# A norm's root made as a row on all partitions in the feed-forward and gate stages of a two-block network

## The chip, the cores and the metric

The kernel runs on one core of a Trainium2 chip. The metric is the device time of one execution in microseconds (us), the median of several runs. The engines are named as the profile names them: PE multiplies matrices, PEld loads its stationary operand, DVE and ACT work on vectors, POOL is GpSimd, SP issues most of the DMAs.

## The reference

A sequence of 256 positions with 1024 features goes through two network blocks. The first has a feed-forward stage, a mixer (neighbourhood attention and pooling), a second feed-forward stage and a gate; the second has a mixer (stick-breaking attention and a convolution), a cross attention to a memory, and a third feed-forward stage. Every stage starts with a norm, and the feed-forward and gate stages look like this:

```python
def rms_norm(x, g):
    xf = x.astype(jnp.float32)
    y = xf * lax.rsqrt(jnp.mean(xf * xf, axis=-1, keepdims=True) + RMS_EPS)
    return (y * g.astype(jnp.float32)).astype(x.dtype)

def swiglu(x, w_gate, w_up, w_down):
    return (jax.nn.silu(x @ w_gate) * (x @ w_up)) @ w_down

f = swiglu(rms_norm(h, ffn1_pre_g[i]), ffn1_w_gate[i], ffn1_w_up[i], ffn1_w_down[i])
h = h + 0.5 * rms_norm(f, ffn1_post_g[i])
...
e = (p[i] @ ple_w_proj[i]) * jax.nn.sigmoid(rms_norm(h, ple_pre_g[i]) @ ple_w_gate[i])
h = h + rms_norm(e, ple_post_g[i])
```

The root is one number for each of the 256 positions. It scales a whole column of a product, so it can be multiplied in after the matmul as well as before it.

## The kernel before

The stream `h` lies transposed in SBUF: features on the 128 partitions in 8 chunks (`DC`), the 256 positions (`T`) along the free axis. Weights come as 345 units of 8 blocks of 128 x 128 floats. `Stream` loads each unit by one DMA into `raw`, ACT rounds it to `wh` (line 90), DVE subtracts to get the remainder `wl` (line 101), and this is issued four units ahead of the unit that PE uses. A product is three matmuls (`mm3`: `wh` by high x, `wl` by high x, `wh` by low x), or two where the moving operand holds both halves of x in 512 columns (`mm2`, `wide`).

Every engine works in the order in which the code issues its instructions; nothing is sorted later. `tick` runs what was put off with `after`. PSUM is five `pm` banks (tile `mm`) and three `pa` banks (tile `at`), taken in turn; a bank is taken again when its last reader is done.

The norm is put off: the matmuls run on `h` times the gain, and the root is multiplied in when a bank is emptied. For it, the squares of the 8 chunks are summed in `acc` (128 x 256). `stat` makes the root as a column: two matmuls of 128 positions each, with one column of ones as the moving operand, put the sums of the positions on partitions; DVE scales 128 x 2 numbers (`v`, line 283), POOL raises them to the power -0.5 (`r`, line 285). `bcast` turns that into a row on all partitions: two matmuls with `r` spread over 128 columns as the stationary operand and the identity as the moving one. `bcast_sb` has ACT copy this row from PSUM to the tile `rs` (line 297).

`ffn` starts with four output pairs at once (`nk` = 4 banks, gate and up half in each) over the 8 chunks. In the last but one chunk (`k == DC - 2`) it calls `stat`; after the last chunk `bcast_sb`, then `evac` four times: DVE multiplies the bank by `rs` (line 445), ACT takes the Silu (line 446), and three later steps make the two halves of `a`. The fifth pair's gate half goes to the fifth bank; its up half needs the first of the four banks again:

```python
            rs = self.bcast_sb(r)
            for m in range(nk):
                evac(m, zt(), bs[m].t)
            for m in range(nk, FC):
                z = zt()
                for sub, (name, off) in enumerate((gate, up)):
                    b = self.bank()
                    self.wide(b, name, off + m, range(DC), x)
```

`ple` (the gate stage) begins likewise with six outputs in three banks, then takes two more in a fourth; `bcast_sb` stands between these two. Its `stages` empty the banks step by step (line 900 multiplies by `rs`) while PE works through `fill`ers, pieces of the memory's key and value products; the last step makes `acc` (line 929) for the `join` behind it, which calls `stat` after four more fillers. `ffn` runs three times, `ple` once. `first_group` in the two mixers, the query stage of the memory, `mem_prep_stat`, `join` and the end of the kernel keep `stat` in both kernels.

The setup allocates a tile `gap` of 128 x 128 floats that nothing uses.

Of the kernel before, what the change touches and what calls it, by code (L numbers as in the profile page):

```python
# [10 lines left out]
F32 = mybir.dt.float32  # L11
F32R = mybir.dt.float32r
AF = mybir.ActivationFunctionType
ALU = mybir.AluOpType

P = 128
T = 256
D = 1024
# [3 lines left out]
EPS = 1e-6  # L22
# [117 lines left out]
class Net:  # L140
# [89 lines left out]
    def setup(self):  # L230
        nc, b, d = self.nc, self.base, self.d
        hg = b.tile([P, G_ALL + DC * T], F32, name="hg")
        self.gv, self.h = hg[:, 0:G_ALL], hg[:, G_ALL:].rearrange("p (c t) -> p c t", c=DC)
        self.x = Split(b.tile([P, DC, 2, T], F32R, name="x"))
        self.fg = b.tile([P, DC, T], F32, name="fg")
        self.ident = b.tile([P, P], F32, name="ident")
        self.ones = b.tile([P, 1], F32, name="ones")
        self.mhalf = b.tile([P, 2], F32, name="mhalf")
        self.half = b.tile([P, 4 * DC], F32, name="half")
        nc.scalar.preload_act_table_set("silu_and_others")  # L240
        at = [(0, 1), (1, 1), (2, 2), (4, 2), (6, 2)]
        for u, (lo, n) in enumerate(at):
            s = slice(G_ALL + lo * T if lo else 0, G_ALL + (lo + n) * T)
            nc.sync.dma_start(out=hg[:, s], in_=d["gx"][:, s])  # L244
            self.ws.load(u, START.get(u, (UB,)))
        nc.gpsimd.memset(self.ones, 1.0)
        nc.gpsimd.memset(self.mhalf, -0.5)
        idle = self.fg[:, 0]
        nc.vector.memset(idle, 0.0)
        w = self.abank()  # L250
        for _ in range(WARM):
            nc.tensor.matmul(w.t[:, 0:T], idle[:, 0:P], idle, start=True, stop=True)
        nc.gpsimd.dma_start(out=self.ident, in_=d["cst"][:, C_ID:C_ID + P])
        b.tile([P, P], F32, name="gap")

    def g(self, name, c):
        i = GAINS.index(name) * DC + c
# [22 lines left out]
    def stat_end(self, b):  # L280
        nc = self.nc
        v = self.tmp.tile([P, 2], F32, tag="v", name="v")
        nc.vector.tensor_scalar(out=v, in0=b.t[:, 0:2], scalar1=1.0 / D, scalar2=EPS, op0=ALU.mult, op1=ALU.add)  # L283
        r = self.tmp.tile([P, 2], F32, tag="r", name="r", bufs=3)
        nc.gpsimd.tensor_tensor(out=r, in0=v, in1=self.mhalf, op=ALU.pow)  # L285
        return r

    def bcast(self, r):

        b = self.abank()  # L290
        for t in range(2):
            self.mm(b, b.t[:, t * P:(t + 1) * P], r[:, t:t + 1].to_broadcast([P, P]), self.ident, stop=True)
        return b.t
# [135 lines left out]
    def ffn(self, gate, up, down, on_chunk, nk=4):  # L429
        nc = self.nc  # L430
        x = self.x
        with self.tc.tile_pool(name="ffn", bufs=1, reuse_waits="tile") as fp:
            self.fp = fp
            a = Split(fp.tile([P, FC, 2, T], F32R, name="a"))
            aH, aL = a[0], a[1]

            def zt():
                return fp.tile([P, 2, T], F32, tag="z", name="z", bufs=6)

            def join2(z, b):  # L440
                nc.scalar.copy(out=z, in_=b.t[:, 1])  # L441
                nc.vector.tensor_tensor(out=z, in0=b.t[:, 0], in1=z, op=ALU.add)  # L442

            def evac(m, z, src):
                nc.vector.tensor_tensor(out=z, in0=src, in1=self.row(rs), op=ALU.mult)  # L445
                nc.scalar.activation(out=z[:, 0], in_=z[:, 0], func=AF.Silu)  # L446

                def s1():
                    nc.vector.tensor_tensor(out=z[:, 0], in0=z[:, 0], in1=z[:, 1], op=ALU.mult)  # L449

                def s2():
                    nc.scalar.copy(out=aH[:, m], in_=z[:, 0])

                def s3():
                    nc.vector.tensor_tensor(out=aL[:, m], in0=z[:, 0], in1=aH[:, m].bitcast(F32), op=ALU.subtract)

                self.after(1, s1)
                self.after(2, s2)
                self.after(3, s3)

            bs = [self.bank() for _ in range(nk)]
            for k in range(DC):
                for m in range(nk):
                    for sub, (name, off) in enumerate((gate, up)):
                        w = self.ws.take(name, k, off + m)
                        self.mm3(bs[m], bs[m].t[:, sub], w, x.at(k), stop=k == DC - 1)
                if k == DC - 2:
                    r = self.stat([self.acc])
                self.tick()
            rs = self.bcast_sb(r)  # L470
            for m in range(nk):
                evac(m, zt(), bs[m].t)
            for m in range(nk, FC):
# [4 lines that stand above are left out]
                    join2(z[:, sub], b)  # L478
                    if sub == 1:
                        evac(m, z, z)  # L480
                    self.tick()
            for c in range(DC):
                b = self.bank()
                two = c < DC - 1
                for k in range(FC):
                    w = self.ws.take(down, k, c)
                    if two:
                        self.mm2(b, w, a.at(k), stop=k == FC - 1)
                    else:
                        self.mm3(b, b.t[:, 0], w, a.at(k), stop=k == FC - 1)  # L490
                    if k % 8 == 4:
                        self.tick()
                on_chunk(c, b.t[:, 0], b.t[:, 1] if two else None)
# [386 lines left out]
    def ple(self, fill):  # L880
        nc = self.nc
        x = self.x
        gp = self.halved(2, "ple_post_g", 0.5)
        bs = [self.bank() for _ in range(3)]
        for k in range(DC):
            for j in range(6):
                w = self.ws.take("ple_w_gate", k, j)
                self.mm3(bs[j // 2], bs[j // 2].t[:, j % 2], w, x.at(k), stop=k == DC - 1)
            if k == DC - 2:
                r = self.stat([self.acc])  # L890
            self.tick()
        fg = self.fg
        qs = []
        off = (0, 0, 0, 1)

        def stage(i, j):
            s = slice(2 * j, 2 * j + 2)
            f = fg[:, s]
            if i == 0:
                nc.vector.tensor_tensor(out=f, in0=bs[j].t, in1=self.row(rs), op=ALU.mult)  # L900
            elif i == 1:
                nc.scalar.activation(out=f, in_=f, func=AF.Tanh, scale=0.5)
            elif i == 2:
                nc.vector.scalar_tensor_tensor(out=f, in0=f, scalar=1.0, in1=self.pp[:, s], op0=ALU.add, op1=ALU.mult)
            elif i == 3:
                q = self.plez.tile([P, 2, T], F32, tag="pq", name="pq", bufs=4)
                nc.scalar.activation(out=q, in_=f, func=AF.Square, scale=0.5)
                qs.append(q)
            elif i == 4:
                if j:  # L910
                    nc.vector.tensor_tensor(out=qs[0], in0=qs[0], in1=qs[j], op=ALU.add)

        def stages(n):
            for j in range(4):
                if 0 <= n - off[j] < 5:
                    stage(n - off[j], j)

        bs.append(self.bank())
        for i in range(2):
            self.proj(bs[3], i, "ple_w_gate", 6 + i, range(DC), x)  # L920
            if i == 0:
                rs = self.bcast_sb(r)
            stages(i)
            self.tick()
        for n in range(2, 6):
            self.fill(fill)
            stages(n)
        self.acc = self.new_acc()
        nc.vector.tensor_tensor(out=self.acc, in0=qs[0][:, 0], in1=qs[0][:, 1], op=ALU.add)
        return gp  # L930
# [532 lines left out]
```

## Time and profile before

| | |
|---|---|
| median of 3 runs | 1034.66 us (1033.92 to 1034.78) |
| the profiled execution's own time | 1036.4 us |
| its span, first to last instruction | 1034.6 us |
| PE busy | 1024.7 us (99%) |
| DVE busy | 760.9 us (74%) |
| ACT busy | 585.1 us (57%) |
| POOL busy | 44.9 us (4%) |
| mean granted TensorE clock | 0.998 |

The span is shorter than the execution's time by 1.8 us. Times in the rows below count from the start of the span. A matmul's record is longer than the matmul's share of PE, since matmuls overlap: what one costs is read from the distance between two starts. An fp32 matmul of the program stands as two records in the trace, one of the rounded kind as one.

### The profile page before, as it was taken

The numbers are of one execution on the slowest core, as the hardware profiler recorded it, in microseconds if no ns is written. First come the engines' busy times: TensorE is split into PE (matmuls) and PEld (weight loads), VectorE is DVE, ScalarE is ACT, GpSimd is POOL, SyncE is SP. The second block draws the span as 40 slices with busy tenths as digits, with TensorE's granted clock in tenths as the row PEclk, the third lists the DMA queues.
The fourth block names the chain that finished last, engine by engine and source line by source line (L and its number), as shares of the span: only waits on it lengthen the run. The fifth ranks groups of instructions, "written<-read, shape, count | busy, mean of one in ns | idle before, by whom it ended". The sixth has DMA issues, their size and how long they took to land.

```text
span 1034.6 us, 18209 instructions
## 1 busy us (share of the span) xinstructions
PE 1024.7 (99%) x7272; PEld 963.9 (93%) x7272; DVE 760.9 (74%) x1200; ACT 585.1 (57%) x981; POOL 44.9 (4%) x73
## 2 busy tenths in 40 slices
PE   9999999999999999999999999999999999999996
PEld 8988888999999998888889999999999999888886
DVE  7798864687858679888457776886678677878652
ACT  7566654464654556556456565465556555656531
POOL 0100000120000110000000111000001000000000
PEclk9999999999999999999999999999999999999999
DMA  8566665455555655666655665555566346666541
GB/s 299 191 218 213 186 206 197 175 191 180 197 162 163 208 203 164 204 187 183 203 183 183 194 201 195 163 163 163 159 222 231 105 140 198 211 187 187 183 156 42
DMA packets 55014, 191.35 MB, mean 185 GB/s; under 512 B 6400, under 2 KB 7936, under 8 KB 54928
## 3 DMA queue, kind: packets, MB, share of 16 engines
q1 hardware_dynamic: 52848, 184.11, 54.7%
q0 software_dynamic: 1936, 5.80, 1.9%
q8 instruction: 57, 0.93, 0.4%
q14 instruction: 29, 0.24, 0.1%
q10 hardware_dynamic: 144, 0.26, 0.1%
HBM read 187.00 MB, written 3.15 MB: 184 GB/s over the span
## 4 chain that ended last, share of the span: by engine, by line
PE 82%; issue 16%; DMA 0%; POOL 0%; DVE 0%; SPq 0%; POOLq 0%; DVEq 0%; ACT 0%
PE mm L197 79%; PE at L197 3%; PE at L875 1%; DMA raw<-ws 0%; POOL r L285 0%; DVE fg L1373 0%; POOLq L1456 0%; DVEq L1456 0%; SPq L63 0%; ACT wh L78 0%; SPq L244 0%; DVE v L283 0%
## 5 line engine op out<-in xcount | busy, mean ns | idle before, releaser
L197 PE MATMUL mm<-x,wh 128*128 128x256 f32 (+1 forms) x2784 | 654.1, 316 | 0.7 <-ACT wh L78 0.7
L197 PE MATMUL mm<-x,wl 128*128 128x256 f32 x1824 | 513.6, 282 | 0.0
L197 PEld LDWEIGHTS mm<-x,wh 128*128 128x128 f32 x2784 | 462.2, 189 | 36.1 <-ACT wh L78 1.6
L101 DVE TENSOR_TENSOR wl<-raw,wh 128x1024 fp32r<-128x1024 f32 x340 | 409.7, 1219 | 11.6 <-ACT wh L90 5.9
L90 ACT CAST wh<-raw 128x1024 fp32r<-128x1024 f32 x340 | 349.0, 1046 | 37.7 <-PE mm L197 22.6
L197 PEld LDWEIGHTS mm<-x,wl 128*128 128x128 f32 x1824 | 345.5, 189 | 1.2 <-DVE wl L79 0.4
L197 PE MATMUL mm<-a,wh 128*128 128x512 f32 (+1 forms) x594 | 185.2, 368 | 0.0
L197 PE MATMUL mm<-a,wl 128*128 128x256 f32 x528 | 147.5, 280 | 0.0
L197 PEld LDWEIGHTS mm<-a,wh 128*128 128x128 f32 x594 | 107.2, 188 | 19.1
L197 PEld LDWEIGHTS mm<-a,wl 128*128 128x128 f32 x528 | 99.2, 188 | 0.0
L446 ACT ACTIVATE z<-z 128x256 f32<-128x256 f32 x66 | 27.2, 418 | 80.6 <-DVE z L445 80.6
L442 DVE TENSOR_TENSOR z<-mm,z 128x256 f32<-128x256 f32 x108 | 45.5, 421 | 29.9 <-ACT z L441 29.8
L441 ACT COPY z<-mm 128x256 f32<-128x256 f32 x108 | 39.6, 367 | 32.9 <-PE mm L197 32.7
L307 ACT ACTIVATE x<-hg 128x256 fp32r<-128x256 f32 x56 | 27.5, 537 | 41.6 <-DVE hg L380 22.1
L285 POOL TENSOR_TENSOR r<-v,mhalf 128x2 f32<-128x2 f32 x13 | 18.5, 1422 | 679.8 <-DVE v L283 679.8
L445 DVE TENSOR_TENSOR z<-z,rs 128x512 f32<-128x512 f32 x54 | 37.4, 692 | 1.8
L352 DVE TENSOR_TENSOR fg<-mm,fg 128x256 f32<-128x256 f32 x14 | 5.9, 425 | 40.7 <-ACT fg L351 40.7
L449 DVE TENSOR_TENSOR z<-z 128x256 f32<-128x256 f32 x66 | 27.2, 424 | 8.1 <-ACT z L446 1.9
L311 DVE SCALAR_TENSOR_TENSOR x<-hg,x 128x256 fp32r<-128x256 f32 x56 | 26.8, 515 | 6.6 <-ACT x L307 6.6
L351 ACT COPY fg<-mm 128x256 f32<-128x256 f32 x14 | 5.2, 373 | 42.0 <-PE mm L197 42.0
L326 DVE TENSOR_TENSOR acc<-acc,sq 128x256 f32<-128x256 f32 x27 | 11.5, 426 | 23.6 <-ACT sq L325 23.5
L197 PE MATMUL mm<-y,wh 128*128 128x256 f32 x136 | 27.7, 283 | 0.0
(218 smaller groups left out, 1033.0 us busy)
## 6 DMA issues: line engine op xcount, KB each, us to landing
raw<-ws SPq DMA_DIRECT2D x340, 512.0 KB, 4.1
raw<-ws SPq DMA_DIRECT2D x9, 256.0 KB, 5.3
ub<-ub SPq DMA_DIRECT2D x8, 160.0 KB, 2.8
mraw<-memT POOLq DMA_DIRECT2D x8, 128.0 KB, 4.3
kd<-kv POOLq DMA_DIRECT2D x8, 128.0 KB, 3.6
vd<-kv POOLq DMA_DIRECT2D x4, 256.0 KB, 4.5
kv<-kd POOLq DMA_DIRECT2D x4, 256.0 KB, 5.9
kv<-vd POOLq DMA_DIRECT2D x4, 256.0 KB, 6.7
```

Of the source, the lines that this page charges most:

```text
L90: self.nc.scalar.copy(out=h, in_=self.R[self.nhigh])
L101: self.nc.vector.tensor_tensor(out=l, in0=self.R.pop(u), in1=self.H[u].bitcast(F32), op=ALU.subtract)
L197: self.nc.tensor.matmul(out, lhsT, rhs, start=not b.started, stop=stop, skip_group_check=True)
L285: nc.gpsimd.tensor_tensor(out=r, in0=v, in1=self.mhalf, op=ALU.pow)
L307: self.nc.scalar.activation(out=self.ordered(x[0][:, c]), in_=self.rows(self.h[:, c]), func=AF.Copy, scale=gain(c))
L311: self.nc.vector.scalar_tensor_tensor(out=l, in0=self.rows(self.h[:, c]), scalar=gain(c), in1=h, op0=ALU.mult, op1=ALU.subtract)
L326: nc.vector.tensor_tensor(out=acc, in0=acc, in1=s, op=ALU.add)
L441: nc.scalar.copy(out=z, in_=b.t[:, 1])
L442: nc.vector.tensor_tensor(out=z, in0=b.t[:, 0], in1=z, op=ALU.add)
L445: nc.vector.tensor_tensor(out=z, in0=src, in1=self.row(rs), op=ALU.mult)
L446: nc.scalar.activation(out=z[:, 0], in_=z[:, 0], func=AF.Silu)
L449: nc.vector.tensor_tensor(out=z[:, 0], in0=z[:, 0], in1=z[:, 1], op=ALU.mult)
```

## The change

`stat_all` is a new function: one matmul has a 128 x 128 square of ones as its stationary operand and `acc` (256 columns) as the moving one, so that the sums of all positions stand as a row on every partition. DVE scales 128 x 256 numbers from PSUM into the tile `rs`, and POOL raises this tile to the power -0.5 in place. `ffn` and `ple` call it in the last but one chunk where they called `stat`, and no longer call `bcast_sb`. The tile of ones takes the place of `gap`, and POOL fills it once in the setup.

```diff
-        b.tile([P, P], F32, name="gap")
+        self.square1 = b.tile([P, P], F32, name="square1")
+        nc.gpsimd.memset(self.square1, 1.0)
...
+    def stat_all(self, a):
+
+        nc = self.nc
+        b = self.abank()
+        self.mm(b, b.t[:, 0:T], self.square1, a, stop=True)
+        t = self.tmp.tile([P, T], F32, tag="rs", name="rs", bufs=1)
+        nc.vector.tensor_scalar(out=t, in0=b.t[:, 0:T], scalar1=1.0 / D, scalar2=EPS, op0=ALU.mult, op1=ALU.add)
+        nc.gpsimd.tensor_tensor(out=t, in0=t, in1=self.mhalf[:, 0:1].to_broadcast([P, T]), op=ALU.pow)
+        return t
...
                 if k == DC - 2:
-                    r = self.stat([self.acc])
+                    rs = self.stat_all(self.acc)
                 self.tick()
-            rs = self.bcast_sb(r)
             for m in range(nk):
...
             if k == DC - 2:
-                r = self.stat([self.acc])
+                rs = self.stat_all(self.acc)
             self.tick()
...
             self.proj(bs[3], i, "ple_w_gate", 6 + i, range(DC), x)
-            if i == 0:
-                rs = self.bcast_sb(r)
             stages(i)
```

What stands on DVE around the norm of the first feed-forward stage, before (`z<-mm,rs` is `evac`'s product with the root, `z<-mm,z` and `z<-z` its later steps):

```order
L101 TENSOR_TENSOR wl<-raw,wh 128x1024 x6
L283 TENSOR_SCALAR v<-at 128x2
L101 TENSOR_TENSOR wl<-raw,wh 128x1024
L445 TENSOR_TENSOR z<-mm,rs 128x512 x4
L101 TENSOR_TENSOR wl<-raw,wh 128x1024
L442 TENSOR_TENSOR z<-mm,z 128x256
```

The same place in the changed kernel:

```order
L101 TENSOR_TENSOR wl<-raw,wh 128x1024 x6
L295 TENSOR_SCALAR rs<-at 128x256
L101 TENSOR_TENSOR wl<-raw,wh 128x1024
L456 TENSOR_TENSOR z<-mm,rs 128x512 x4
L101 TENSOR_TENSOR wl<-raw,wh 128x1024
L453 TENSOR_TENSOR z<-mm,z 128x256
```

The order is the same; the scaling step has 256 columns where it had 2, and one `wl` still stands between it and the four products.

On POOL, from the first DMA of the setup to the second root (`ISA` is the loading of the power's code, `mraw` a chunk of the memory's input), before:

```order
L253 DMA ident<-cst 128x128
L285 ISA
L285 TENSOR_TENSOR r<-v,mhalf 128x2
L501 DMA mraw<-memT 128x256 x8
L285 TENSOR_TENSOR r<-v,mhalf 128x2 x2
```

The same place in the changed kernel:

```order
L253 DMA ident<-cst 128x128
L255 MEMSET square_114 128x128
L296 ISA
L296 TENSOR_TENSOR rs<-rs,mhalf 128x256
L511 DMA mraw<-memT 128x256 x8
L286 TENSOR_TENSOR r<-v,mhalf 128x2 x2
```

The first power now has 256 columns, and the DMAs of `mraw` stand behind it as they stood behind the small one; the other feed-forward stages and the gate read alike.

## Rows read from the trace of the kernel before

**Rows 1.** First section of the page: busy time, share of the span, instructions.

```profile
PE 1024.7 (99%) x7272; PEld 963.9 (93%) x7272; DVE 760.9 (74%) x1200; ACT 585.1 (57%) x981; POOL 44.9 (4%) x73
```

**Rows 2.** Waits of PE, all of them: total us, times, longest.

```profile
PE at L252 <- DVE fg L249: 1.2, 1, 1.2
PE at L197 <- ACT sq L1284: 0.8, 1, 0.8
PE mm L197 <- ACT wh L78: 0.7, 1, 0.7
```

**Rows 3.** Timeline of PE at the first norm: start, length, instruction, records.

```profile
28.86 0.50 PE L197 MATMUL at<-ones,acc 128*128 128x1 f32 x4
29.22 0.36 PE L197 MATMUL mm<-x,wh 128*128 128x256 f32 x1
29.42 0.28 PE L197 MATMUL mm<-x,wl 128*128 128x256 f32 x1
...
32.11 0.61 PE L197 MATMUL at<-ident,r 128*128 128x128 f32 x4
32.47 0.48 PE L197 MATMUL mm<-x,wh 128*128 128x512 f32 x1
32.79 0.28 PE L197 MATMUL mm<-x,wl 128*128 128x256 f32 x1
32.91 0.39 PE L197 MATMUL mm<-x,wh 128*128 128x512 f32 x1
...
34.99 0.39 PE L197 MATMUL mm<-x,wh 128*128 128x512 f32 x1
...
35.33 0.39 PE L197 MATMUL mm<-x,wh 128*128 128x512 f32 x1
```

**Rows 4.** Timeline of PE in the second mixer, an fp32 256-column and 128-column matmul.

```profile
654.47 0.87 PE L197 MATMUL mm<-qz,kT 128*128 128x256 f32 x4
655.09 0.36 PE L197 MATMUL mm<-x,wh 128*128 128x256 f32 x1
```

**Rows 5.** DVE: timeline at the first norm, then one group of lines by form.

```profile
29.39 0.16 DVE L283 TENSOR_SCALAR v<-at 128x2 f32<-128x2 f32 x1 [3.13 <-PE at L197]
29.50 1.23 DVE L101 TENSOR_TENSOR wl<-raw,wh 128x1024 fp32r<-128x1024 f32 x1
33.16 2.49 DVE L445 TENSOR_TENSOR z<-mm,rs 128x512 f32<-128x512 f32 x4 [2.43 <-ACT rs L297]
...
L442 DVE TENSOR_TENSOR z<-mm,z 128x256 f32<-128x256 f32 x108 | 45.5, 421 | 29.9 <-ACT z L441 29.8
```

**Rows 6.** POOL: line 285 (ns min/median/max), its first instruction, two memsets by form.

```profile
L285 POOL TENSOR_TENSOR r<-v,mhalf x13: 692/1600/1661, 29.7 to 1027.2; 128x2 f32<-128x2 f32 x13
...
29.71 1.60 POOL L285 TENSOR_TENSOR r<-v,mhalf 128x2 f32<-128x2 f32 x1 [27.69 <-DVE v L283]
...
L609 POOL MEMSET vz<- 128x512 f32 x4 | 2.2, 608 | 0.0
...
L246 POOL MEMSET ones<- 128x1 f32 x1 | 0.1, 98 | 0.3 <-POOLq L1453 0.3
```

**Rows 7.** The gate stage: timeline of DVE, and PE at the next norm.

```profile
572.02 0.16 DVE L283 TENSOR_SCALAR v<-at 128x2 f32<-128x2 f32 x1 [0.81 <-PE at L197]
572.12 2.36 DVE L101 TENSOR_TENSOR wl<-raw,wh 128x1024 fp32r<-128x1024 f32 x2
577.80 1.89 DVE L900 TENSOR_TENSOR fg<-mm,rs 128x512 f32<-128x512 f32 x3 [3.32 <-ACT rs L297]
...
589.60 0.43 DVE L929 TENSOR_TENSOR acc<-pq 128x256 f32<-128x256 f32 x1
...
592.21 0.50 PE L197 MATMUL at<-ones,acc 128*128 128x1 f32 x4
```

**Rows 8.** DVE, line 101: ns min/median/max of all its instructions.

```profile
L101 DVE TENSOR_TENSOR wl<-raw,wh x340: 1208/1219/1237, 19.1 to 1012.2; 128x1024 fp32r<-128x1024 f32 x170
```

**Rows 9.** Stretches: length, busy us of each engine (records), granted clock, DMA.

```profile
10.00:12.00 2.00, 2.00 (x11) 2.00 (x11) 1.77 (x3) 1.72 (x4) 0.00 (x0) 1.00 1.05 377
26.00:32.00 6.00, 6.00 (x54) 6.00 (x53) 1.60 (x3) 2.10 (x2) 2.29 (x3) 1.00 0.87 310
```

## The prediction

> **What bounds the kernel now.** I read the busy times first: PE is busy 99% of the span, POOL 4% [rows 1]. Then the waits: PE waited three times, 2.7 us in all, never at one of the norms that change [rows 2]. So PE's own work sets the end. A matmul taken off PE is worth its share in full; whatever makes PE wait costs in full; faster work on the other engines is worth nothing. The waits of DVE at these norms [rows 5, 7] cost nothing today, because PE has work meanwhile. What matters is how long the root may take before PE has none.
>
> **PE's work.** There are four places: three feed-forward stages and the gate. I read prices as distances between starts, and count the late start of the matmul behind, since two neighbours are normally 0.12 us apart (32.79 to 32.91) [rows 3]. The two narrow matmuls of the old sum take 29.22 - 28.86 = 0.36 us, and the step behind them is 0.20 in place of 0.12: 0.44. The two broadcast matmuls take 32.47 - 32.11 = 0.36, and the 512-column matmul behind them keeps PE 0.32 where another keeps it 0.23 (34.99 to 35.33 holds a pair, 0.34, less 0.12): 0.45 with rounding. Together 0.89. The new matmul is fp32, 256 columns, with a 128-column stationary operand. Its nearest row is the pair in the mixer: one of 256 and one of 128 columns take 655.09 - 654.47 = 0.62 [rows 4]; half of the broadcast's 0.36 is the share of the 128-column one, so 0.44 is left, and 0.08 for the step behind: 0.52. The saving is 0.37 a place, four times: **1.5 us**. ACT's copy of the row goes too; PE did not wait for it, so it counts as nothing by itself. The 128 x 128 memset in the setup costs POOL, by the memsets [rows 6], under 0.25 us near the start, where POOL then idles 27.69 us until 29.71: nothing. The changed positions of SP's DMAs: none.
>
> **DVE's step.** Scaling 256 columns from PSUM in place of 2: the nearest row is a 256-column step that reads PSUM, 0.42 us [rows 5], against 0.16. That is 0.26 later for the `wl` behind it, which is made four units ahead and hides it.
>
> **The power's price.** With 2 columns it takes 0.69 us where DVE lets it; the median of 1.60 is longer only because of a wait: the first one starts at 29.71, beside a `wl` from 29.50 to 30.73, and ends at 31.31, that is 0.58 after the `wl` [rows 5, 6]. Nothing in the trace has more than 2 columns of it, so the price of one more column, call it c, is bounded from both sides. Lower end: a memset's column, (608 - 98)/511 = 1.0 ns [rows 6]; the power would then take 0.69 + 254 x 0.001 = 0.95 us. Upper end: all of 0.69 beyond the memset's 0.10 of handling belongs to the two columns, 0.295 us each, and 256 of them take 75.6 us. It cannot be a gain. The ends are a factor of 80 apart. The row nearest in kind is the power itself, and it says that 0.59 us lies beyond what handling costs a memset, so the function is not cheap; but two columns also pay once for whatever filling of a pipe there is, so the full upper end is not likely either. I take the geometric middle, sqrt(0.95 x 75.6) = 8.5 us, that is **c = 31 ns** and 254 c = 7.8 us beyond the small power. This is the one number of the forecast that I choose rather than read.
>
> **How much of it is hidden in a feed-forward stage.** Replayed with the rows of the first norm [rows 3, 5, 6]. The new matmul ends 0.08 later than the old pair, so DVE's scaling starts at 29.39 + 0.08 = 29.47 and ends at 29.89. The `wl` behind it starts 0.05 earlier than that (29.50 against 29.55 today), 29.84, and ends at 31.07. The power ends 0.58 after it plus 254 c: 31.65 + 254 c. `evac`'s first product waits for that, takes a fourth of 2.49 with its overlaps, 0.69 us for one (2.49 less three starts 0.60 apart), and frees the first bank at about 32.4 + 254 c. PE, without the broadcast, starts the fifth pair at 32.11 + 0.08 = 32.19; its gate half is 8 pairs of 0.345, (35.33 - 32.47 - 0.10)/8, so PE wants the first bank at 34.95. The wait is 254 c - 2.5 us. The other two feed-forward stages have the same order and the same distances within 0.1 us. With 254 c = 7.8 each waits 5.3, **15.9 us** for three. Queued behind the waiting product: on DVE the other three products and the next `wl`, on ACT the four Silus and the next rounding, on POOL the DMAs of `mraw` and `kv`, wanted much later. The weights are four units ahead, 32 blocks of 0.35 us or 11 us, so this lateness does not add to the wait for the bank; the later banks come free every 0.6 us while PE needs 2.8 for each.
>
> **The gate.** Here the scaling would run from 572.10 to 572.52, the first `wl` to 573.70 and the power to 574.28 + 254 c. DVE's first product stands at 577.80 today, since it waited for the broadcast. From there DVE works nearly without a gap until `acc` at 590.03, and PE asks for it at 592.21 [rows 7], which is 2.2 to spare. So 577.80 + 2.18 - 574.31 = 5.7 us of 254 c are hidden. With 7.8, PE waits **2.1 us**. PE's bank for its second filler comes free earlier than that and is no limit.
>
> One more way to lose time: POOL and DVE can stand in each other's way. The rows show one direction, the power waited for `wl`'s end [rows 5, 6]. The other does not show: all 340 `wl` took 1.208 to 1.237 us, also those that ran beside a power [rows 8]. The Trainium skill, "SBUF — State Buffer", section "SBUF: two separate sides", says that whoever starts first holds the pair for the whole instruction and the other is blocked. By it the gate's second `wl` would stand behind the power and add 1.2 us there; the row speaks against it, and the sum has nothing for it.
>
> **PE's pace after a wait.** At the start of the program PE ran 11 records in 2 us, 5.5 a us, where later it runs 54 in 6, 9.0 a us [rows 9]; the column of the granted clock reads 1.00, the level of 2.4 GHz, in both. If a wait of 5 us brought that slow pace back for as long as the wait was, each would cost 5.3 x 3.5/9.0 = 2.1 us more. No row has a wait inside the work, so the bounds are 0 and 2.1; I take 0, because the clock's column shows no fall, and keep the other end for the range (up to 8 us for four).
>
> **The sum.** 15.9 + 2.1 - 1.5 = +16.5 us. Against the profiled execution's own 1036.4 us (span 1034.6) that is 1052.9; that execution was 1.7 us above the median of the runs, so for a median I add to 1034.66: **1051.1 us**, slower by 1.6%.
>
> **The rivals.** *The power is hidden.* If c is below 2.5/254 = 10 ns, PE never waits and only the 1.5 us remain: 1033.2, not slower. The mechanism is a pipelined power that pays most of its 0.69 us once. For it: DVE's scaling step has the same shape of price, 0.16 us for 2 columns though 256 take only 0.42. Against it: a memset has only 0.10 to pay once. It decides at c = 10 ns; the balance of gain and loss is at 3 (254 c - 2.5) = 1.5, c = 12 ns. The Trainium skill, "GPSIMD Engine Reference", section "Elementwise — side-by-side cycle accounting", gives about 2.6 cycles at 1.2 GHz for an element of a two-input operation, measured for an addition; an estimate by it is 0.55 us for 256 columns, which would be this rival and 1033.2. No run here shows it for a power. *No overlap between columns.* If half of the 0.59 us is paid per column, c = 148 ns, 254 c = 37.5, three waits of 35.0 and one of 31.8: 1034.66 + 136.8 - 1.5 = 1170; at the full upper end, 254 c = 75, it is 1320. For it: a root by logarithm and exponential is long, and two columns took 0.69. *Partly hidden.* c between 10 and 14 ns leaves the time within 0.2%: three waits of 1.2 against 1.5.
>
> **How the numbers follow.** About 0.2%, 2.07 us, is what a measurement of this kernel can tell from no change. Power hidden or nearly so (c up to 14 ns): 0.38, nearly all of it within 0.2%; faster by more than that needs a saving above 2.07 where the rows give 1.5, so 0.04 of it. The forecast's case, c from 14 to 90 ns: 0.46. Beyond: 0.16. That gives faster 0.04, same 0.34, slower 0.62. At c = 90 ns, 254 c = 22.9, the sum is 61.2 + 17.2 - 1.5 = 76.9, and with a slow pace after some of the waits about 81: the range ends at 1115. It starts at 1032.8, the hidden case with 0.4 for reading errors. What is left out is the last case and the fast tail, 2 in 10.
>
> **What would show it.** In the changed profile, the power's row gives c at once. Right: PE waits at three places for DVE's product with `rs`, each 254 c - 2.5, and less at the gate's next norm; DVE's idle time at that line goes to POOL. The saving would show as four pairs of broadcast matmuls gone, and starts of the new matmul 0.44 before the next one. Wrong: a power under 3.2 us and no wait of PE; or waits of PE for `wl`, a slower pace behind a wait, or longer `wl` beside the power.

## The result and the profile after

The changed kernel takes 1187.46 us (median of 5 runs, 1186.59 to 1188.93) against 1034.39 of the kernel before: a ratio of 1.1486, 95% interval 1.1474 to 1.1498. That is 153.1 us more, outside the range that was given. The direction was right, the size was not.

The page of the changed kernel, first section (busy time, share, instructions) and the chain that ended last, to be read beside [rows 1]:

```profile
PE 1030.6 (87%) x7248; PEld 967.1 (81%) x7248; DVE 762.3 (64%) x1200; ACT 584.6 (49%) x977; POOL 206.6 (17%) x74
...
PE 69%; POOL 14%; issue 14%; DVE 1%; DMA 0%; SPq 0%; POOLq 0%; DVEq 0%; ACT 0%
```

PE's busy time hardly moved; it stood still for 13% of the span. POOL works 162 us more, and one line of it is 14% of the chain. The waits of PE in the changed kernel (total us, times, longest), beside [rows 2]:

```profile
PE mm L197 <- DVE z L456: 113.5, 3, 37.9
PE mm L197 <- DVE fg L910: 32.9, 1, 32.9
```

These are the three feed-forward stages and the gate: 146.4 us of waiting that was not there. The power itself (ns min/median/max) and the first of the four places on POOL, DVE and PE, each from its timeline:

```profile
L296 POOL TENSOR_TENSOR rs<-rs,mhalf x4: 41992/41998/42055, 28.5 to 971.5; 128x256 f32<-128x256 f32 x4
...
28.46 42.00 POOL L296 TENSOR_TENSOR rs<-rs,mhalf 128x256 f32<-128x256 f32 x1 [26.20 <-DVE rs L295]
...
70.50 2.49 DVE L456 TENSOR_TENSOR z<-mm,rs 128x512 f32<-128x512 f32 x4 [41.06 <-POOL rs L296]
...
71.33 0.76 PE L197 MATMUL mm<-x,wh 128*128 128x512 f32 x1 [37.91 <-DVE z L456]
72.11 0.63 PE L197 MATMUL mm<-x,wh 128*128 128x512 f32 x1
72.75 0.63 PE L197 MATMUL mm<-x,wh 128*128 128x512 f32 x1
...
75.11 0.39 PE L197 MATMUL mm<-x,wh 128*128 128x512 f32 x1
75.45 0.39 PE L197 MATMUL mm<-x,wh 128*128 128x512 f32 x1
```

256 columns of power take 42.0 us. DVE's product, PE's bank and PE's next matmul follow one behind the other, as the prediction had put it. Behind the wait the pairs of matmuls stand 0.64 us apart, not 0.345, until about 75. The stretches there (length, busy us of PE, PEld, DVE, ACT, POOL with records, then the granted clock, the DMA's share and its GB/s) say why:

```profile
36.00:70.00 34.00, 0.00 (x0) 0.00 (x0) 0.00 (x0) 0.00 (x0) 34.00 (x1) 0.52 0.00 0
...
72.00:74.00 2.00, 2.00 (x8) 1.71 (x7) 2.00 (x3) 1.64 (x4) 0.11 (x1) 0.50 0.63 178
74.00:76.00 2.00, 2.00 (x11) 1.77 (x10) 1.44 (x5) 1.59 (x3) 0.00 (x0) 0.79 0.39 72
76.00:80.00 4.00, 4.00 (x25) 3.54 (x24) 3.48 (x7) 1.71 (x6) 0.00 (x0) 1.00 0.55 177
```

The granted clock fell to 0.50, the level of 1.2 GHz, while PE stood still, and it was still there for the first matmuls.

### The profile page after: what moved, and what is told of

It reads as the page before. It is cut to its first block, busy times and chain, and to the rows that moved or that the text cites. A ratio compares the mean times of both kernels' runs of the same rounds, so it can differ in the third digit from the quotient of the medians.

```text
span 1186.7 us, 18164 instructions
## 1 busy us (share of the span) xinstructions
PE 1030.6 (87%) x7248; PEld 967.1 (81%) x7248; DVE 762.3 (64%) x1200; ACT 584.6 (49%) x977; POOL 206.6 (17%) x74
## 4 chain that ended last, share of the span: by engine, by line
PE 69%; POOL 14%; issue 14%; DVE 1%; DMA 0%; SPq 0%; POOLq 0%; DVEq 0%; ACT 0%
PE mm L197 66%; POOL rs L296 14%; PE at L197 3%; PE at L885 0%; DMA raw<-ws 0%; DVE wl L101 0%; DVE fg L914 0%; DVE fg L910 0%; DVE pq L921 0%; DVE rs L295 0%; POOL r L286 0%; DVE z L456 0%; SPq L63 0%; DVE fg L1381 0%; POOLq L1464 0%
## 5 line engine op out<-in xcount | busy, mean ns | idle before, releaser
L296 POOL TENSOR_TENSOR rs<-rs,mhalf 128x256 f32<-128x256 f32 x4 | 168.0, 42010 | 101.5 <-DVE rs L295 101.5
L286 POOL TENSOR_TENSOR r<-v,mhalf 128x2 f32<-128x2 f32 x9 | 11.9, 1320 | 573.6 <-DVE v L284 573.6
L456 DVE TENSOR_TENSOR z<-mm,rs 128x512 f32<-128x512 f32 x12 | 7.5, 684 | 123.2 <-POOL rs L296 123.2
L197 PE MATMUL mm<-wh,m 128*128 128x256 f32 x128 | 25.5, 297 | 32.9 <-DVE fg L910 32.9
L197 PEld LDWEIGHTS mm<-wh,m 128*128 128x128 f32 x128 | 21.4, 202 | 33.1 <-DVE fg L910 33.1
```

Source lines behind the costliest of these rows:

```text
L197: self.nc.tensor.matmul(out, lhsT, rhs, start=not b.started, stop=stop, skip_group_check=True)
L296: nc.gpsimd.tensor_tensor(out=t, in0=t, in1=self.mhalf[:, 0:1].to_broadcast([P, T]), op=ALU.pow)
```

## The experiments

The theory: all of the loss is the power's price per column, through the waits for the bank and the low clock behind them; the rest of the change is a small gain. The rivals: making the row on POOL costs by itself; the replay of what is hidden was wrong too; the slow pace behind the waits is weights that come late.

**Multiply instead of power.**

```diff
-        nc.gpsimd.tensor_tensor(..., op=ALU.pow)
+        nc.gpsimd.tensor_tensor(..., op=ALU.mult)
```

> The changed kernel with GpSimd's power replaced by a multiplication of the same 256 columns (so the root is left out and the output differs). Theory, the power's price per column is the whole loss and the rest of the change saves 1.5 us on PE: 1032.9 us, no wait of PE at the four places, GpSimd's instruction under 2 us. Rival, the loss lies in making the row on GpSimd at all (its reads beside VectorE, or the wait on one more engine in the chain): still above 1036, with a wait of PE for the product with rs.

Measured: 1032.42 us against 1034.46, a ratio of 0.998 (0.9971 to 0.9988). PE does not wait at any of the four places. Line 296 of this kernel:

```profile
L296 POOL TENSOR_TENSOR rs<-rs,mhalf x4: 609/1450/1512, 28.2 to 856.4; 128x256 f32<-128x256 f32 x4
```

The same columns in the same place on the same engine take 0.61 us when the function is a product: that is the first of the four, which starts before the `wl`; the other three start beside a running `wl` and take 1.45 to 1.51, as the small power did. So POOL, its reads and the further wait in the chain are not the loss; the function is. The first rival falls.

**Powers of four sizes, off the path.**

```diff
-        b.tile([P, P], F32, name="gap")
+        gap = b.tile([P, P], F32, name="gap")
+        nc.gpsimd.memset(gap, 0.7)
+        for n in (2, 2, 16, 64):
+            nc.gpsimd.tensor_tensor(out=gap[:, 0:n], in0=gap[:, 0:n], in1=self.mhalf[:, 0:1].to_broadcast([P, n]), op=ALU.pow)
```

> The kernel before, with four powers that nobody reads in GpSimd's idle time at the start, of 2, 2, 16 and 64 columns in this order. Theory, a fixed part and a constant price per column: 42.0 us for 256 and 0.69 for 2 give 0.163 us a column, so 0.69, 0.69, 3.0 and 10.8 us; the time stays at 1034.4 within 1 us, since nobody waits. Rival, a price that grows in steps or a cost of the first call: 16 columns below 1.5 us, or the first power longer than the second by 1 us or more. Second rival, a power holds back VectorE's two-input instructions for its whole length: wl instructions beside it of 3 to 10 us, and a time above 1036.

Measured: 1034.22 us, ratio 0.9999 (0.999 to 1.0009). POOL's groups by form (busy us, mean ns):

```profile
L257 POOL TENSOR_TENSOR gap<-gap,mhalf 128x64 f32<-128x64 f32 x1 | 10.8, 10797 | 0.1
L257 POOL TENSOR_TENSOR gap<-gap,mhalf 128x16 f32<-128x16 f32 x1 | 2.9, 2948 | 0.1
L257 POOL TENSOR_TENSOR gap<-gap,mhalf 128x2 f32<-128x2 f32 x2 | 1.4, 710 | 0.2
```

From 2 to 16 columns it is (2.948 - 0.710)/14 = 0.160 us a column, from 16 to 64 (10.797 - 2.948)/48 = 0.164: a straight line with some 0.38 us paid once. No cost of the first call shows. The same line gives 42.2 us at 256 columns. Nobody waits for these powers and they cost nothing. The second rival falls too: the eleven `wl` of line 79 ran beside these powers and took 0.43 to 0.69 us, in the kernel before 0.42 to 0.69.

**A power of 48 columns.** It takes nearly the time that the prediction assumed, so it tests everything but the price.

```diff
-        nc.gpsimd.tensor_tensor(out=t, in0=t, in1=self.mhalf[:, 0:1].to_broadcast([P, T]), op=ALU.pow)
+        nc.gpsimd.tensor_tensor(out=t[:, 0:48], in0=t[:, 0:48], in1=self.mhalf[:, 0:1].to_broadcast([P, 48]), op=ALU.pow)
```

> The changed kernel with the power on the first 48 of the 256 columns only (the other columns keep the mean square, so the output differs). At 0.163 us a column this power takes 8.2 us, 7.5 beyond the small one, nearly what the prediction chose. Theory, the prediction's replay of the stages was right and its price was wrong: waits of PE of 5.0 us at three places and about 1.8 at the gate, less 1.5 of saving: 1050, up to 1057 if PE runs slowly behind each wait. Rival, the replay hides less or more than it said (a wait comes 2 us earlier, or the later banks and weights add to it): below 1045 or above 1060.

Measured: 1055.2 us, ratio 1.0201 (1.0187 to 1.0215). The waits of PE in this kernel, and two stretches around the first of them:

```profile
PE mm L197 <- DVE z L456: 14.4, 3, 5.0
PE at L197 <- DVE acc L937: 1.9, 1, 1.9
...
34.00:36.00 2.00, 0.00 (x0) 0.00 (x0) 0.00 (x0) 0.00 (x0) 2.00 (x1) 0.82 0.00 0
...
38.00:40.00 2.00, 2.00 (x8) 1.71 (x8) 1.92 (x3) 1.64 (x4) 0.00 (x0) 0.50 0.50 156
```

Three waits of 4.8 on average where 5.0 were expected, and 1.9 at the gate, for `acc`, where 1.8 were. The waits are 16.3 us; less about 2 of gain that leaves some 14, and 1055.2 - 1034.5 = 20.7 were measured. The rest, some 6.4 us, goes to the clock: it falls within a wait of 5 us too, and from the first matmul behind the first wait the next eight pairs took 5.2 us where they take 2.8, which is 2.4 for a wait and 7.2 for three. The replay of the waits holds.

**PE kept busy during the waits**, first with 155 idle matmuls in each of the three feed-forward waits, then with 166.

```diff
                     self.wide(b, name, off + m, range(DC), x)
+                    if m == nk and sub == 0:
+                        w = self.abank()
+                        for _ in range(155):
+                            nc.tensor.matmul(w.t, x.at(0)[0][:, 0:P], x.at(0)[2].rearrange("p a t -> p (a t)"), start=True, stop=True)
```

> The changed kernel with 155 matmuls of 512 columns, read by nobody, in each of the three feed-forward waits, about 35 us each, so that PE is busy nearly until the power ends. Theory, a wait of 38 us costs a further 1.7 us at each place because TensorE's clock has fallen to 1.2 GHz and comes back only later: 1182.3, the granted clock at 1.00 in the first us behind these three waits, and 0.5 behind the gate's wait, which is left as it is. Rival, PE is slow there for another reason (weights or banks that come late): 1187.5 within 1.5 us, and the same distances between matmuls behind the wait.

> As the run with 155 idle matmuls, with 166 of them. There 2.8 us were left idle behind them, and the granted clock fell all the same, so that run could not tell. Now some 0.4 us stay idle. Theory, the slow pace behind the three feed-forward waits is the granted clock's: 1182.3 us (1187.4 less three times 1.7), pairs 0.345 us apart at once behind the wait, the clock at 1.00 there. Rival, late weights or banks: 1187.4 within 1.5 us and pairs 0.64 us apart behind the wait.

Measured: 1187.4 us with 155, no different from the changed kernel; 1181.54 with 166. The first left 2.8 us idle (three waits, 8.1 us in all), and the clock went down all the same; the second left two waits of 0.2. The stretch of 72 to 74 us, first with 155, then with 166, and behind the second the power at this place and the first two pairs:

```profile
72.00:74.00 2.00, 2.00 (x9) 1.71 (x8) 1.96 (x3) 1.64 (x4) 0.00 (x0) 0.50 0.51 154
```

```profile
72.00:74.00 2.00, 2.00 (x13) 1.76 (x13) 1.44 (x3) 2.00 (x4) 0.00 (x0) 1.00 0.36 55
...
28.00 41.16 POOL L296 TENSOR_TENSOR rs<-rs,mhalf 128x256 f32<-128x256 f32 x1 [25.73 <-DVE rs L295]
...
70.44 0.39 PE L197 MATMUL mm<-x,wh 128*128 128x512 f32 x1
...
70.79 0.39 PE L197 MATMUL mm<-x,wh 128*128 128x512 f32 x1
```

With the clock at 1.00 the pairs stand 0.345 us apart at once, with the same weights and banks, and 5.9 us are gone. In the profiled executions 0.8 of them are the first power's, 41.16 us where it takes 42.00 in the changed kernel: here it starts at 28.00, before the `wl` beside it, there at 28.46, behind the start of the `wl` at 28.22. That leaves 1.7 for each wait, and the starts in the changed kernel say the same: the six pairs from 71.33 to 75.11 take 3.78 us in place of 2.07. So the slow pace is the clock's, and the third rival falls. The first of the two runs could not tell: its expectation was wrong in assuming that so short an idle time would not matter.

**A power of 16 columns.**

```diff
-        nc.gpsimd.tensor_tensor(out=t, in0=t, in1=self.mhalf[:, 0:1].to_broadcast([P, T]), op=ALU.pow)
+        nc.gpsimd.tensor_tensor(out=t[:, 0:16], in0=t[:, 0:16], in1=self.mhalf[:, 0:1].to_broadcast([P, 16]), op=ALU.pow)
```

> The changed kernel with the power on the first 16 columns only (the others keep the mean square, so the output differs). This power took 2.95 us by itself, 2.26 beyond the small one, just below the 2.5 us that the prediction found hidden. Theory: PE never waits at the four places, 1032.4 us, as with the multiplication. Rival, less is hidden than the prediction said: a wait of 0.5 us or more at each place and 1034 or more.

Measured: 1031.69 us, ratio 0.9971 (0.996 to 0.9982), no wait of PE at the four places, though each power, with the `wl` that it waits for, lasts 3.8 us. DVE still waited for them, 10.2 us in all; that cost nothing. Together with 48 columns this brackets the point at which a longer power starts to cost: between 16 and 48 columns, where the prediction's 2.5 us put it at about 17.

**The gate alone.** The feed-forward stages go back to `stat` and `bcast_sb`.

```diff
                 if k == DC - 2:
-                    rs = self.stat_all(self.acc)
+                    r = self.stat([self.acc])
                 self.tick()
+            rs = self.bcast_sb(r)
```

> The change in the gate stage alone; the feed-forward stages are those of before. Theory, the four places add up, and the gate's share is its wait of 32.9 us in the changed kernel's trace, 1.7 us of low clock behind it, less 0.5 of saving: 1068.6 us. By the prediction's own replay, with 5.7 us hidden, 254 columns at 0.163 give 35.7 and 1071.4. Rival, the places are not independent: off by more than 3 us from both.

Measured: 1068.12 us, ratio 1.0325 (1.0311 to 1.0339), with the one wait of 32.9 us. That is what was expected if the places add up. The 1071.4 by the prediction's formula is 3.3 too long; the part on the prediction says why.

**The root by ScalarE from the same row.** Does the row form gain where the root is quick?

```diff
-        nc.vector.tensor_scalar(out=t, in0=b.t[:, 0:T], scalar1=1.0 / D, scalar2=EPS, op0=ALU.mult, op1=ALU.add)
-        nc.gpsimd.tensor_tensor(out=t, in0=t, in1=self.mhalf[:, 0:1].to_broadcast([P, T]), op=ALU.pow)
+        nc.scalar.activation(out=t, in_=b.t[:, 0:T], func=AF.Ln, scale=1.0 / D, bias=self.eps)
+        nc.scalar.activation(out=t, in_=t, func=AF.Exp, scale=-0.5)
...
+        self.eps = b.tile([P, 1], F32, name="eps")
+        nc.gpsimd.memset(self.eps, EPS)
```

> The changed kernel with the root made by ScalarE from the row in PSUM, as exp(-0.5 ln(mean + eps)): two activations of 256 columns in place of VectorE's scaling and GpSimd's power. It asks whether the row form gains where the root is quick. Theory: root ready some 3 us after the sum with the loads of ScalarE's tables, before PE wants the bank, so 1032.4 us, faster than before by 0.2%. Rival, the table loads or the rounding of weights behind them on ScalarE make PE wait: 1034 or more, with a wait of PE for wh or for the product with rs.

Measured: 1046.39 us, ratio 1.0113 (1.01 to 1.0127), outside what was expected: PE did not wait at the four places. Its matmuls were further apart, also in stages that the edit does not touch. The edit has a side effect: the new tile of 4 bytes a partition moves the tiles allocated behind it (by the order of the code; the traces show no addresses). Two runs took that apart. The first puts the constant into an unused column of `half`; the second is the kernel before with a 4-byte tile and nothing else:

```diff
-        self.eps = b.tile([P, 1], F32, name="eps")
+        self.eps = self.half[:, 4 * DC - 1:4 * DC]
```

```diff
         b.tile([P, P], F32, name="gap")
+        b.tile([P, 1], F32, name="gap2")
```

> ScalarE's root as in the run before, with its constant of 4 bytes a partition in an unused column of a tile that is there anyway, so that no other tile moves. That run had no wait of PE at the four places, yet its matmuls stood 2.4% further apart for long stretches (24 of them 2.87 us where another variant has 2.80). Theory, the new 4-byte tile moved all tiles behind it and that made matmuls slower; without it 1031.7 us, as with a power of 16 columns, and the output is complete: faster than before by 0.27%. Rival, the table loads or ScalarE's order are what cost: 1044 or more again.

> The kernel before with one unused tile of 4 bytes a partition allocated behind the unused 128 x 128 tile, and nothing else. Theory, that the move of the tiles is the whole cost: about 1034.4 + 14 = 1048 us, matmuls 2 to 3% further apart in the same stretches, no new wait. Rival, ScalarE is the cause: 1034.4 within 1 us.

Measured: 1033.1 us without the move, ratio 0.9989 (0.998 to 0.9998); 1041.92 for the kernel before with the move, ratio 1.0077 (1.0064 to 1.0091). One stretch of 180 matmuls in the first mixer, from the chain (start, length), in the kernel before without the move and then with it:

```profile
227.31 21.23 PE mm L197 x180
```

```profile
225.80 21.75 PE mm L197 x180
```

2.4% slower with nothing else changed. So the move costs, but in the kernel before it costs 7.8 us, and between the two versions with ScalarE it is 13.3. The traces show where the difference lies: the 504 matmuls of the first feed-forward stage, with ScalarE without the move and then with it, are

```profile
29.42 86.01 PE mm L197 x504
```

```profile
29.35 87.69 PE mm L197 x504
```

In the kernel before, the 480 matmuls there take 83.21 us with the move and without. Why the move slows this stage in the one kernel and not in the other stays open. The version without the move computes everything and is faster than the kernel before by 1.1 us, 0.1%, by an interval that just leaves out no change. ScalarE loads a table three times at the first place, 1.28 us each, all hidden behind PE's work.

## Why the prediction was wrong

**The step that failed** is the price of a column, "c = 31 ns". It is 159 ns, five times as much: the power of 256 columns beside a `wl`, 42.0 us, less the small power beside a `wl`, 1.60, is 40.4 us for 254 columns, where 7.8 were forecast. (The 0.163 us of the expectations is 42.0 less 0.69 and counts the delay by the `wl` in.) The two rows that bounded it were right, 1.0 and 295 ns, and the choice between them was not. The geometric middle of two bounds is no reading of a row. The row of the same operation was there: 0.69 us for two columns, of which handling explains 0.10. The second rival had read it that way, with half of the 0.59 us paid per column: 148 ns and 1170 us. It got a chance of 0.16, and the range ended at 1115, below it. Its half was a choice too, and that it came so near is luck; but it started from the nearest row, as the other terms of the sum did.

**The replay of the waits held; the low clock was left out.** With 254 c = 40.4 the prediction's own formulas give 3 x 37.9 + 34.7 - 1.5 = 146.9, or 1181.6, for 1187.46 measured. What is left is mostly the low clock behind the waits, which the sum put at nothing; the smaller terms below partly cancel. Point by point:

- The wait of a feed-forward stage, 254 c - 2.5: 37.9 by the formula, 37.8 measured. With 48 columns the power takes 8.9 us, 7.3 more than 1.60: 4.8 by the formula and 4.8 measured.
- The gate, 254 c - 5.7: 1.6 by the formula and 1.9 measured with 48 columns. With 256 it is 32.9, not 34.7, for another reason than named: PE stands at the bank of its second filler, which the prediction said "is no limit". That filler starts, in the kernel before and then in the changed one, at

```profile
582.85 0.28 PE L197 MATMUL mm<-wh,m 128*128 128x256 f32 x1
```

```profile
692.07 0.58 PE L197 MATMUL mm<-wh,m 128*128 128x256 f32 x1 [32.87 <-DVE fg L910]
```

  The bank leaves 582.85 - 574.31 - 0.7, about 8 us, before it stops PE: no limit at 7.8, the first one at 40.4. Behind it `acc` costs only 0.2 more.
- The low clock: "the bounds are 0 and 2.1; I take 0". It cost 1.7 us behind a wait of 37.9 and 2.4 behind one of 5.0. So it did not grow with the wait, as the 2.1 assumed, and that this bound comes near is luck. The reason given for 0, that the clock's column shows no fall, was no reason: the kernel before has no wait of that kind in which it could have fallen. Its slow start, on which the 2.1 rests, runs at the pace that is found behind the waits. Three matmuls of 256 columns, which are as many columns as a pair has, take 0.64 us there and later 0.35, though the clock's column reads 1.00 from 10 to 12 us [rows 9]:

```profile
10.10 0.63 PE L197 MATMUL mm<-x,wh 128*128 128x256 f32 x2
...
10.74 0.63 PE L197 MATMUL mm<-x,wh 128*128 128x256 f32 x2
...
13.19 0.40 PE L197 MATMUL mm<-x,wh 128*128 128x256 f32 x2
...
13.54 0.40 PE L197 MATMUL mm<-x,wh 128*128 128x256 f32 x2
```

  Why the column does not show the slow pace at the start is open.
- The saving on PE: 0.37 a place was predicted. From one place's sum to the next sum, the kernel before took 86.90 us (29.02 to 115.92 in its chain) and the ScalarE version 86.44 (28.98 to 115.42), so 0.46; the new matmul holds the chain for 0.43 where 0.52 was expected. Four places make 1.8 us, and the measured gains where the root was quick are 2.0, 2.8 and 1.1. One reason that they do not agree better may be the program's start: the first sum stands between 25.96 and 28.86 us in the profiled executions, ahead of anything that the variants change on PE. What sets it was not tried.
- The weights "four units ahead" did cover the lateness: no wait of PE for a weight shows behind the waits.

The estimate by the Trainium skill's "GPSIMD Engine Reference", section "Elementwise — side-by-side cycle accounting", 0.55 us for 256 columns, agrees with the product's 0.61 here and says nothing of a power: that takes 69 times as long.

## What to carry to other kernels

A function's price per column cannot be read exactly off two columns, but here the row of the same function was a better guide than the middle between two bounds; where one number decides and its bounds are a factor of 80 apart, the range has to reach to where that row points. Making a small tensor wide, here 2 columns into 256 so that no broadcast is needed, pays 254 times for whatever is not cheap per element, and is worth trying only on an engine where the function is cheap per column, as the product was here. When PE sets the end and must wait, add to the wait what its clock costs behind it, here 1.7 to 2.4 us.

## What the runs showed of the hardware

- GpSimd's power costs 0.16 us for each column of 128 partitions, from 2 columns to 256 (42.0 us); a product of 256 columns costs 0.61 us in all, where no `wl` delays it.
- The granted clock went to 0.50 in idle times of 38 and of 5.0 us and just behind those of 2.8 us, and stayed at 1.00 where some 0.2 us were idle at a time. Behind a wait the low clock cost 1.7 to 2.4 us.
- A power of 42 us does not hold VectorE back for its length. The longest `wl` of the changed kernel, the second one at the gate, was held by 0.41 us and ran beside the power; compare [rows 8]:

```profile
L101 DVE TENSOR_TENSOR wl<-raw,wh x340: 1210/1219/1634, 19.4 to 1164.3; 128x1024 fp32r<-128x1024 f32 x170
```

  The Trainium skill's "SBUF — State Buffer", section "SBUF: two separate sides", has the loser blocked for the whole instruction. The measurement differs: 0.41 of 42.0 us.
- One more tile of 4 bytes a partition, allocated ahead of others, made some runs of matmuls 2.4% slower (180 in 21.75 us for 21.23), others not at all (480 in 83.21), and the kernel before 7.8 us longer. An edit that allocates a tile changes more than it says; a comparison should keep the addresses of the rest.
